# Pricing tile-size changes and holding small tiles in a build-time scheduler: a two-layer hybrid decoder on one Trainium2 core

## The chip, the cores and the metric

The kernel runs on one core of one Trainium2 chip. The metric is device time in microseconds, the median of three runs. TensorE (PE) multiplies, VectorE (DVE), ScalarE (ACT) and GpSimd (POOL) work elementwise, SyncE (SP) issues the DMAs. The kernel is one program with a queue of instructions for each engine. The order in each queue is fixed when the kernel is built, and semaphores make one engine wait for another.

## The reference

Two layers over a sequence of 512 tokens of width 1024, batch 1. Each layer is a mixer of three branches and a gated MLP with a short convolution, both between normalisations whose scales come from a condition `c` ("ada"):

```python
def token_mixer(h, ...):
    z = h @ w_in
    za, zb, zc, zg = split(z)
    y_a = nsa_attention(...)     # sparse: compressed, selected and window keys; 8 heads of 64
    y_b = mla_branch(...)        # low-rank q and kv, 8 heads of 96
    y_c = rwkv7_branch(...)      # recurrent state, 8 heads of 64, group norm
    g_a, g_b, g_c = split(sigmoid(zg))
    merged = g_a * (y_a @ w_a) + g_b * (y_b @ w_b) + g_c * (y_c @ w_c)
    return merged @ w_out

def conv_ffn(h, w_up, conv_w, conv_b, w_down):
    gate, val = split(causal_dwconv(h @ w_up, conv_w, conv_b))
    return (gelu(gate) * val) @ w_down

def reference(x, c, ...):
    for l in range(2):
        h = rms_norm(x, gain0) * (1 + sc1) + sh1
        x = x + gt1 * rms_norm(token_mixer(h, ...), gain1)
        h = rms_norm(x, gain2) * (1 + sc2) + sh2
        x = x + gt2 * rms_norm(conv_ffn(h, ...), gain3)
    return x
```

All arithmetic is float32.

## The kernel before, in words

**Two kinds of work.** The products with the weights (w_in, w_branch, w_out, ffn_up, ffn_down) form one long stream. A weight chunk is loaded by DMA (`rawt`), split by ACT (L507) and DVE (L476) into a high and a low half (`hlt`), and multiplied as three matmuls: high with high, high with low, low with high. These three are one stream operation; there are 2384 of them, and most of their matmuls have 512 columns. They run in one task, `master`, spawned under the name "gemm". Everything else is small: products of attention heads, of the RWKV pairs and of compression, most with 64 or 32 rows or columns, and the transposes (`tr`, L463, 128x128). Each stands in a task of its own: `mla_head` and `mla_pair`, `nsa_pair`, `rwkv_pair`, `pre` (normalise and transpose one of the four token tiles, 128 tokens each) and `post` (the residual step ahead of it).

**Tile sizes.** TensorE works in tiles of 128, 64 or 32 rows by 128, 64 or 32 columns, by the partitions of the stationary operand and by its width. The stream and the transposes use 128x128, the small products mostly 64x64, some 128x64, 64x128 and 32x32. In the profile the size stands behind the names (`64*64`).

**Who sets the order.** `Sched.run` simulates all engines while the program is built and picks one operation at a time. An operation's key begins with its earliest start (when its operands are ready by the planner's costs and its engine is free), then comes the task's priority (0 to 3 for small tasks, 9 for the stream: lower goes first), then its number. So a small product that the planner holds to be ready goes ahead of the stream, and the stream fills the rest. The costs (`pe`, L457, and `tr`) and the latencies between engines (`LAT`) are planned values; on the chip an engine waits when the planned order asks for something that is late.

**The places that matter here.** The stream is cut into units. Those of a branch ("BR") wait until all the branch's heads are done, by `yield ev("y", l, br)`; for MLA (branch 1) that is the end of the last `mla_pair`, and its first unit in layer 0 begins at stream operation 296 (B10 below), in layer 1 at 1504. `mla` spawns its heads two at a time, numbers 104 to 111 in layer 0; each takes four logits products, four row minima on DVE (`soft_head`, L1797), four exponentials on ACT, four normalisations on DVE (L485), transposes, and products with the values. In `rwkv_pair` the last pair ("rw3") ends with a chain of 128x512 elementwise steps on DVE (L476), then four transposes. `ada_block` makes the modulation vectors; three of its adds at a time run on POOL (L971). At the start of the MLP ("UP") and of layer 1, `post` and `pre` of the four token tiles feed the stream's first units (`first_units`: first the half with token tiles 0 and 1, then that with 2 and 3); the scaling by the norm is L1185, what leaves the transposes' PSUM bank is L1211 (ACT) and L1213 (DVE).

Of the kernel before, what the change touches and what calls it, by code (L numbers as in the profile page):

```python
# [58 lines left out]
class Ev:  # L59
    def __init__(self):  # L60
        self.deps = None


class Op:
    __slots__ = ("engs", "nbytes", "cols", "bank")

    def __init__(self, engs, nbytes=0, cols=0.0, bank=None):
        self.engs = engs
        self.bank = bank
        self.nbytes = nbytes  # L70
        self.cols = cols


class Cond:
    __slots__ = ("f",)
# [12 lines left out]
class Alloc:  # L88
    __slots__ = ("mem", "n", "cls", "job")
# [5 lines left out]
class Reserve:  # L95
    __slots__ = ("mem", "job")
# [111 lines left out]
}  # L208
FREE = 150.0


class Task:
    __slots__ = ("gen", "prio", "deps", "base", "req", "done", "name", "seq")
# [16 lines left out]
class Sched:  # L230


    def __init__(self):
        self.t = {e: 0.0 for e in ("PE", "ACT", "DVE", "POOL", "SP")}
        self.dma = 0.0
        self.tasks = []
        self.ticks = {}
        self.fill = None
        self.fill_t = 0.0
        self.cool = False  # L240
        self.past = []
        self.cur = None
        self.nseq = 0
        self.now = 0.0
        self.seen = {}
# [36 lines left out]
    def _step(self, k, val):  # L282
# [6 lines left out]
            k.req = None  # L289
        self.cur = prev  # L290

    TICK = 10240.0 / 3
    SHARE = 5000.0
    WARM = 3400.0
# [30 lines left out]
    def run(self):  # L325
        while self.tasks:
            best = None
            for k in self.tasks:
                r = k.req
                if type(r) is Op:  # L330
                    for e, c in r.engs:
                        st = max(k.at(e), self.t[e])
                        if r.bank in self.seen:

                            end, other = self.seen[r.bank]
                            if other != e:
                                st = max(st, end + LAT[other][e])
                        if k is self.fill and self.cool and (st > self.fill_t + self.SHARE or self.cooling(st)):
                            key = (st, -2, k.seq, 0.0)
                        elif len(r.engs) > 1:  # L340
                            key = (st, k.prio, k.seq, st + c)
                        else:
                            key = (st, k.prio, k.seq, 0.0)
                        if best is None or key < best[0]:
                            best = (key, k, e, c, st)
                    continue
                if type(r) is Ev:
                    if r.deps is None:
                        continue
                    st, e = max(k.ready(), max([t for t, g in r.deps])), None  # L350
                    key = (st, -1, k.seq, 0.0)
                elif type(r) is Cond:
                    if not r.f():
                        continue
                    st, e = max(k.ready(), self.now), None
                    key = (st, -1, k.seq, 0.0)
                elif type(r) is Reserve:
                    if not r.mem.reserve(r.job):
                        continue
                    st, e = max(k.ready(), self.now), None  # L360
                    key = (st, k.prio, k.seq, 0.0)
                else:
                    f = r.mem.find(r.n, r.cls, k.ready(), r.job)
                    if f is None:
                        continue
                    e, st = f
                    key = (st, k.prio - 0.5, k.seq, 0.0)
                if best is None or key < best[0]:
                    best = (key, k, e, 0.0, st)
# [6 lines left out]
            _, k, e, c, st = best  # L376
            self.now = max(self.now, st)
            r = k.req
            if type(r) is Op:
                end = self.pe_time(st, c, r.cols) if e == "PE" else st + c  # L380
                self.t[e] = end
                if r.bank is not None:
                    self.seen[r.bank] = (end, e)
# [23 lines left out]
def _fsz(ap):  # L407
    n = 1
    for s in ap.shape[1:]:
        n *= s  # L410
    return n
# [18 lines left out]
class Kern:  # L430
# [11 lines left out]
    def pe(self, mms, share=1.0):  # L442
        cost = cols = 0.0
        for out, lhsT, rhs, st, sp in mms:
            n, m = _fsz(rhs), _fsz(lhsT)
            if lhsT.dtype == FR:
                cost += max(n / 2.4, m / 1.2) + 3
                cols += n * lhsT.shape[0] * min(m, 128) / 16384
            else:
                c = max(n / 0.6, m / 0.684)  # L450
                if m <= 64:
                    c = (n / 0.6 + 47) / 2 if n > 16 else 53
                cost += c
                cols += 4 * n * lhsT.shape[0] * min(m, 128) / 16384
        yield Op([("PE", cost * share)], cols=cols)
        for out, lhsT, rhs, st, sp in mms:
            self.nc.tensor.matmul(out, lhsT, rhs, start=st, stop=sp)  # L457

    def tr(self, trs):
        cost = sum(0.85 * _fsz(ident) + 2 for _, _, ident in trs)  # L460
        yield Op([("PE", cost)], cols=sum(2 * _fsz(i) * i.shape[0] / 128 for _, _, i in trs))
        for out, in_, ident in trs:
            self.nc.tensor.transpose(out, in_, ident)  # L463

# [2308 lines left out]
```

## Time and profile before

| | |
|---|---|
| times of the runs | 2071.28, 2071.88, 2068.06 us, median 2071.28 |
| profiled execution | 2071.48 us, of which the span is 2069.4 us |
| mean granted TensorE clock | .994 |
| PE busy | 2019.6 us (98%) |
| DVE / ACT / POOL busy | 1340.3 / 998.2 / 292.2 us |
| PE's share of the chain that ended last | 88%, DVE 8% |
| largest group | L457 128x512 of `arenar,hlt`, 2880 matmuls, 711.7 us |

How to read it: the span is the time from the first instruction to the last; 2.1 us lie around it in this execution. A PE that is busy 98% is the bound, and what can be gained is what its queue loses: waits, changes of tile, and stretches at half clock (`PEclk` is the clock that was granted, 1.00 is full). Consecutive matmuls overlap, so the pace of a group is read from the starts of rows, not from the mean duration of one instruction.

### The profile page before, as it was taken

The numbers are of one execution on the slowest core, as the hardware profiler recorded it, in microseconds if no ns is written. First come the engines' busy times: TensorE is split into PE (matmuls) and PEld (weight loads), VectorE is DVE, ScalarE is ACT, GpSimd is POOL, SyncE is SP. The second block draws the span as 40 slices with busy tenths as digits, with TensorE's granted clock in tenths as the row PEclk, the third lists the DMA queues.
The fourth block names the chain that finished last, engine by engine and source line by source line (L and its number), as shares of the span: only waits on it lengthen the run. The fifth ranks groups of instructions, "written<-read, shape, count | busy, mean of one in ns | idle before, by whom it ended". The sixth has DMA issues, their size and how long they took to land.

```text
span 2069.4 us, 35607 instructions
## 1 busy us (share of the span) xinstructions
PE 2019.6 (98%) x14134; PEld 1638.0 (79%) x14134; DVE 1340.3 (65%) x2754; ACT 998.2 (48%) x1898; POOL 292.2 (14%) x268
## 2 busy tenths in 40 slices
PE   6999999999999999999999999999999999999998
PEld 4887777777788888888888777777777878888887
DVE  6687985677556766662467789765865676656423
ACT  4454652466445656541344456534754455444321
POOL 3001000340030234200010100004302211100000
PEclk9999999999999999999999999999999999999999
DMA  7532212441245355424422221224313544333342
GB/s 308 152 93 74 72 43 87 153 163 52 99 166 173 123 194 174 141 92 141 138 85 67 66 89 57 75 87 166 129 62 123 173 143 168 108 102 93 101 133 81
DMA packets 88423, 245.48 MB, mean 119 GB/s; under 512 B 24984, under 2 KB 26392, under 8 KB 87872
## 3 DMA queue, kind: packets, MB, share of 16 engines
q1 hardware_dynamic: 88256, 243.20, 35.3%
q8 instruction: 111, 1.82, 0.4%
q14 instruction: 56, 0.46, 0.1%
HBM read 233.19 MB, written 12.60 MB: 119 GB/s over the span
## 4 chain that ended last, share of the span: by engine, by line
PE 88%; DVE 8%; issue 1%; ACT 1%; DMA 1%; POOL 1%; DVEq 0%; POOLq 0%; SPq 0%; ACTq 0%
PE ps L457 83%; PE ps L463 4%; DVE xt L476 1%; DVE xt L485 1%; DVE arena L476 1%; DVE xt L1797 1%; DVE xt L480 1%; DVE hlt L476 1%; ACT xt L472 0%; POOL smallt L517 0%; DVE arena L480 0%; DVE arena L1213 0%; DMA arena<-rwd 0%; DVE xt L2561 0%; DMA rwd<-arena 0%
## 5 line engine op out<-in xcount | busy, mean ns | idle before, releaser
L457 PE MATMUL ps<-arenar,hlt 128*128 128x512 f32 (+1 forms) x2880 | 711.7, 396 | 1.6 <-DVE arenar L476 1.4
L457 PEld LDWEIGHTS ps<-arenar,hlt 128*128 128x128 f32 x2880 | 520.6, 190 | 109.1 <-issue 7.3
L476 DVE TENSOR_TENSOR hlt<-rawt,hlt 128x1024 fp32r<-128x1024 f32 (+2 forms) x260 | 312.6, 1202 | 371.1 <-ACT hlt L507 370.0
L457 PE MATMUL ps<-xt,hlt 128*128 128x512 f32 (+1 forms) x2208 | 477.5, 378 | 4.2 <-ACT arena L1211 4.2
L507 ACT CAST hlt<-rawt 128x1024 fp32r<-128x1024 f32 (+3 forms) x263 | 269.4, 1025 | 431.9 <-PE ps L457 323.0
L457 PEld LDWEIGHTS ps<-xt,hlt 128*128 128x128 f32 x2208 | 397.0, 190 | 81.0 <-ACT arena L1211 4.7
L457 PE MATMUL ps<-hlt,arenar 128*128 128x512 f32 (+3 forms) x1056 | 222.5, 365 | 0.0
L457 PEld LDWEIGHTS ps<-hlt,arenar 128*128 128x128 f32 x1056 | 185.4, 189 | 27.4 <-issue 1.0
L507 ACT COPY xt<-ps 128x512 f32<-128x512 f32 (+6 forms) x211 | 91.0, 476 | 91.6 <-PE ps L457 43.4
L480 DVE SCALAR_TENSOR_TENSOR yt<-ps,cpk,yt 128x511 f32<-128x511 f32 (+1 forms) x160 | 119.5, 747 | 3.3
L457 PE MATMUL ps<-xt 64*64 64x64 f32 (+11 forms) x1992 | 117.1, 258 | 4.3 <-ACT xt L472 2.4
L457 PEld LDWEIGHTS ps<-xt 64*64 64x64 f32 (+6 forms) x1992 | 84.2, 135 | 46.3 <-issue 31.4
L472 ACT ACTIVATE xt<-xt,smallt 128x512 f32<-128x512 f32 (+3 forms) x168 | 92.5, 552 | 55.8 <-DVE smallt L1797 55.7
L517 POOL TENSOR_TENSOR smallt<-smallt,mhalf 128x1 f32<-128x1 f32 (+2 forms) x56 | 58.5, 1049 | 276.3 <-DVE smallt L487 157.1
L457 PE MATMUL ps<-arenar 128*128 128x512 f32 x384 | 93.0, 390 | 0.0
L522 POOL TENSOR_SCALAR smallt<-smallt 128x1 f32<-128x1 f32 x20 | 5.1, 256 | 593.6 <-DVE smallt L487 582.6
L971 POOL TENSOR_TENSOR arena<-xt,arena 128x512 f32<-128x512 f32 x51 | 73.7, 1445 | 71.9 <-issue 36.7
L457 PEld LDWEIGHTS ps<-arenar 128*128 128x128 f32 x384 | 71.7, 188 | 14.7
L463 PE MATMUL ps<-kpack,xt 128*128 128x128 f32 x533 | 73.7, 275 | 6.2 <-DVE xt L476 4.5
L457 PE MATMUL ps<-hlt,xt 128*128 128x512 f32 x336 | 76.8, 389 | 0.0
L463 PEld LDWEIGHTS ps<-kpack,xt 128*128 128x128 f32 x533 | 61.1, 140 | 18.3 <-issue 3.7
L457 PEld LDWEIGHTS ps<-hlt,xt 128*128 128x128 f32 x336 | 63.1, 188 | 13.1
(264 smaller groups left out, 2490.4 us busy)
## 6 DMA issues: line engine op xcount, KB each, us to landing
rawt<-in_wch_dram SPq DMA_DIRECT2D x90, 512.0 KB, 3.5
rawt<-in_wup_dram SPq DMA_DIRECT2D x88, 512.0 KB, 3.5
rawt<-in_wdn_dram SPq DMA_DIRECT2D x44, 512.0 KB, 3.5
arena<-in_wada_dram SPq DMA_DIRECT2D x42, 512.0 KB, 5.2
xt<-in_wada_dram SPq DMA_DIRECT2D x33, 512.0 KB, 5.3
rawt<-in_wbr_dram SPq DMA_DIRECT2D x24, 512.0 KB, 3.5
yt<-in_wada_dram SPq DMA_DIRECT2D x21, 512.0 KB, 4.7
rawt<-in_wout_dram SPq DMA_DIRECT2D x16, 512.0 KB, 3.5
```

The lines of the kernel that those rows point to most:

```text
L457: self.nc.tensor.matmul(out, lhsT, rhs, start=st, stop=sp)
L463: self.nc.tensor.transpose(out, in_, ident)
L472: self.nc.scalar.activation(out, in_, func, bias=bias, scale=scale, **kw)
L476: self.nc.vector.tensor_tensor(out, a, b, op)
L480: self.nc.vector.scalar_tensor_tensor(out, a, s, b, op0, op1)
L485: self.nc.vector.tensor_scalar(out, a, s1, None, op0)
L507: self.nc.scalar.copy(out, in_)
L517: self.nc.gpsimd.tensor_tensor(out, in_, ex, OP.pow)
L522: self.nc.gpsimd.tensor_scalar(out, ss, a, b, OP.mult, OP.add)
L971: self.nc.gpsimd.tensor_tensor(a, w, a, OP.add)
L1797: nc.vector.tensor_tensor_reduce(dst, B3(o), B3(mask_ap(qt)), scale, 3.0e38, OP.add, OP.min, sm[:, qt:qt + 1])
```

## The change

The planner gets to know the tile size of each PE operation (`pe` works it out from the first product, `tr` is always 128x128) and keeps that of the last one in `self.tile`. Three things follow from it and one does not:

- An operation of another size than the last is charged 165 ns (CHANGE) in the planner's clock.
- While the last one was not full size, an operation of another size has 330 ns added to its key: small tiles of one size are held together. Where keys are equal, the one that needs no change goes first.
- A PE operation that is not of the stream counts as ready 150 ns later in its key (LATE). Its start in the planner's clock stays as it was.
- The planned cost of one stream matmul is n/2.4+13.4 ns instead of n/2.4+3, and its bound by weight loading is m/2.4 instead of m/1.2.

No instruction is added or taken away on PE: the program has 11225 matmuls and transposes in both. What changes is the order, and through it the buffers.

```diff
+FULL = (128, 128)
+CHANGE = 165.0
...
+    LATE = 150.0
...
+                        if e == "PE":
+
+                            new = r.tile != self.tile
+                            late = 2 * CHANGE if new and self.tile != FULL else 0.0
+                            if k is self.fill and self.cool and (st > self.fill_t + self.SHARE or self.cooling(st)):
+                                key = (st, -2, k.seq, 0.0)
+                            else:
+
+                                sure = st if k is self.fill else max(k.at(e) + self.LATE, self.t[e])
+                                key = (sure + late, k.prio, new, k.seq)
+                            if best is None or key < best[0]:
+                                best = (key, k, e, c, st)
+                            continue
+                        if len(r.engs) > 1:
...
-                end = self.pe_time(st, c, r.cols) if e == "PE" else st + c
+                if e == "PE":
+                    if r.tile != self.tile:
+                        st, self.tile = st + CHANGE, r.tile
+                    end = self.pe_time(st, c, r.cols)
+                else:
+                    end = st + c
...
-                cost += max(n / 2.4, m / 1.2) + 3
+                cost += max(n / 2.4, m / 2.4) + 13.4
...
+        size = lambda n: 128 if n > 64 else 64 if n > 32 else 32
+        tile = (size(mms[0][1].shape[0]), size(_fsz(mms[0][1])))
+        yield Op([("PE", cost * share)], cols=cols, tile=tile)
...
+        yield Op([("PE", cost)], cols=sum(2 * _fsz(i) * i.shape[0] / 128 for _, _, i in trs), tile=FULL)
```

In the whole PE order the tile size changes 401 times before and 373 times in the change. Three places show what moves. The line numbers are those of each kernel's own file (a matmul is L457 before and L481 in the change, a transpose L463 and L487); `ps_76` to `ps_83` are the eight PSUM banks, and x3 counts matmuls in a row.

First, PE in layer 0, the logits of the sparse branch against the compressed keys (64x31) and beside them stream operations (`arenar,hlt`). Before:

```order
L457 MATMUL ps_77<-arenar,hlt 128x512 x3
L457 MATMUL ps_78<-xt_104 32x32 x16
L457 MATMUL ps_79<-arena 64x31 x2
L457 MATMUL ps_79<-arena,xt_104 64x31 x2
L457 MATMUL ps_79<-arena 64x31 x4
L457 MATMUL ps_77<-arenar,hlt 128x512 x3
L457 MATMUL ps_79<-arena 64x31 x2
L457 MATMUL ps_79<-arena,xt_104 64x31 x2
L457 MATMUL ps_79<-arena 64x31 x4
```

The same kind of rows in the change, which stand later in the stream:

```order
L481 MATMUL ps_76<-arena,xt_104 64x31 x2
L481 MATMUL ps_76<-arena 64x31 x2
L481 MATMUL ps_78<-arenar,hlt 128x512 x3
L481 MATMUL ps_80<-arenar,hlt 128x512 x3
L481 MATMUL ps_79<-arena,xt_104 64x31 x2
L481 MATMUL ps_79<-arena 64x31 x2
```

The stream goes between the small products after a whole bank of them, two operations at a time, where before it went in after one.

Second, PE in layer 0 at the end of MLA. Before, its last products with the values (64x512 to 64x128) stand among stream operations, and 46 more stream operations lie between the last of them and B10:

```order
L457 MATMUL ps_78<-arena,xt_104 64x512 x2
L457 MATMUL ps_78<-arena,xt_104 64x384 x2
L457 MATMUL ps_78<-arena,xt_104 64x256 x2
L457 MATMUL ps_77<-arenar,hlt 128x512 x3
L457 MATMUL ps_76<-xt_104,arena 64x128 x2
L457 MATMUL ps_79<-xt_104,arena 64x128 x2
```

In the change; the first two rows are transposes of the last heads' softmax, the row with `ones` is a norm of rw3, and the last row is the first of B10:

```order
L487 MATMUL ps_83<-kpack,xt_104 128x128 x3
L487 MATMUL ps_79<-kpack,xt_104 128x128 x3
L481 MATMUL ps_76<-xt_104 64x512 x2
L481 MATMUL ps_76<-xt_104 64x384 x2
L481 MATMUL ps_78<-xt_104 64x512 x2
L481 MATMUL ps_79<-ones,arena 64x1 x8
L481 MATMUL ps_76<-xt_104 64x256 x2
L481 MATMUL ps_78<-xt_104 64x384 x2
L481 MATMUL ps_76<-xt_104 64x128 x2
L481 MATMUL ps_78<-xt_104 64x256 x2
L481 MATMUL ps_78<-xt_104 64x128 x2
L481 MATMUL ps_76<-arenar,hlt 128x512 x12
```

The second half of MLA (heads 108 to 111) has moved back by 56 stream operations on average, to the very end of its room; rw3 has moved forward by 22 on average and its last step from stream operation 313 to 296.

Third, PE at the start of the MLP in layer 0: transposes of token tiles (L463, L487) among the first UP units (128x256). Before:

```order
L457 MATMUL ps_76<-xt_5553,hlt 128x256 x24
L463 MATMUL ps_77<-kpack,arena 128x128 x2
L463 MATMUL ps_78<-kpack,arena 128x128 x2
L463 MATMUL ps_80<-kpack,arena 128x128 x2
L463 MATMUL ps_81<-kpack,arena 128x128 x2
L457 MATMUL ps_79<-xt_5553,hlt 128x256 x24
L457 MATMUL ps_77<-xt_5553,hlt 128x256 x9
L463 MATMUL ps_78<-kpack,arena 128x128 x2
```

In the change:

```order
L481 MATMUL ps_76<-xt_5554,hlt 128x256 x24
L487 MATMUL ps_77<-kpack,yt_5235 128x128 x2
L487 MATMUL ps_78<-kpack,yt_5235 128x128 x2
L487 MATMUL ps_79<-kpack,yt_5235 128x128 x2
L487 MATMUL ps_80<-kpack,yt_5235 128x128 x2
L481 MATMUL ps_81<-xt_5554,hlt 128x256 x3
L487 MATMUL ps_82<-kpack,yt_5235 128x128 x2
L487 MATMUL ps_83<-kpack,yt_5235 128x128 x2
L487 MATMUL ps_77<-kpack,yt_5235 128x128 x2
L481 MATMUL ps_81<-xt_5554,hlt 128x256 x3
L487 MATMUL ps_78<-kpack,yt_5235 128x128 x2
```

Of the four transposed tiles the third (t = 2) keeps its place behind 24 products; the fourth (t = 3) came after 33 more products and now comes after 3. It is the same in layer 1.

More of the change, by code (lines that the diff above doesn't have):

```diff
@@ L64, with __init__ @@
 class Op:
-    __slots__ = ("engs", "nbytes", "cols", "bank")
-    def __init__(self, engs, nbytes=0, cols=0.0, bank=None):
+    __slots__ = ("engs", "nbytes", "cols", "bank", "tile")
+    def __init__(self, engs, nbytes=0, cols=0.0, bank=None, tile=None):
         self.engs = engs
@@ L71, in __init__ @@
         self.cols = cols
+        self.tile = tile
 class Cond:
@@ L239, in __init__ @@
         self.fill_t = 0.0
+        self.tile = FULL
         self.cool = False
@@ L337, in run @@
                                 st = max(st, end + LAT[other][e])
-                        if k is self.fill and self.cool and (st > self.fill_t + self.SHARE or self.cooling(st)):
-                            key = (st, -2, k.seq, 0.0)
-                        elif len(r.engs) > 1:
+                        if e == "PE":
[10 more added lines that the diff above has]
+                        if len(r.engs) > 1:
                             key = (st, k.prio, k.seq, st + c)
@@ L454, in pe @@
                 cols += 4 * n * lhsT.shape[0] * min(m, 128) / 16384
-        yield Op([("PE", cost * share)], cols=cols)
+        size = lambda n: 128 if n > 64 else 64 if n > 32 else 32
+        tile = (size(mms[0][1].shape[0]), size(_fsz(mms[0][1])))
+        yield Op([("PE", cost * share)], cols=cols, tile=tile)
         for out, lhsT, rhs, st, sp in mms:
@@ L460, in tr @@
         cost = sum(0.85 * _fsz(ident) + 2 for _, _, ident in trs)
-        yield Op([("PE", cost)], cols=sum(2 * _fsz(i) * i.shape[0] / 128 for _, _, i in trs))
+        yield Op([("PE", cost)], cols=sum(2 * _fsz(i) * i.shape[0] / 128 for _, _, i in trs), tile=FULL)
         for out, in_, ident in trs:
```

## The prediction

> **What bounds the kernel now.** I read the page first, then PE's waits, then the chain and single stretches of the timeline.
>
> ```profile
> span 2069.4 us, 35607 instructions
> PE 2019.6 (98%) x14134; PEld 1638.0 (79%) x14134; DVE 1340.3 (65%) x2754; ACT 998.2 (48%) x1898; POOL 292.2 (14%) x268
> PE 88%; DVE 8%; issue 1%; ACT 1%; DMA 1%; POOL 1%; DVEq 0%; POOLq 0%; SPq 0%; ACTq 0%
> ```
>
> PE is the bound, and the change leaves its work as it is. It can win only where PE loses time: in tile changes, waits and half clock. The pace of the stream stands in the chain (start, us, count of matmuls):
>
> ```profile
> 554.48 114.49 PE ps L457 x506
> ```
>
> 114.49/506 = 0.226 us for each 128x512 matmul. What PE waited for in the whole span (total, times, longest):
>
> ```profile
> PE ps L463 <- DVE yt L1130: 10.7, 2, 7.8
> PE ps L463 <- DVE arena L1185: 6.9, 3, 2.6
> PE ps L463 <- DVE xt L476: 4.5, 4, 1.9
> PE ps L457 <- ACT arena L1211: 4.2, 2, 2.2
> ```
>
> The first row lies at the beginnings of the layers, rows two and four where the four token tiles enter the MLP and layer 1, row three at the ends of rw3. None of these lies in MLA: there the stream covers everything. So these waits are where a new order can take or give.
>
> **Tile changes.** The trace of before has excursions from the stream to 64x64 and back, a run inside 64x64, and one to transposes, which are full size:
>
> ```profile
> 182.49 0.33 PE L457 MATMUL ps<-arena 64*64 64x64 f32 x4
> 182.75 1.67 PE L457 MATMUL ps<-arenar,hlt 128*128 128x512 f32 x6
> 184.35 0.33 PE L457 MATMUL ps<-arena 64*64 64x64 f32 x4
> ...
> 210.91 1.63 PE L457 MATMUL ps<-arenar,hlt 128*128 128x512 f32 x6
> 212.37 0.60 PE L463 MATMUL ps<-kpack,arena 128*128 128x128 f32 x4
> 212.73 2.32 PE L457 MATMUL ps<-arenar,hlt 128*128 128x512 f32 x9
> ...
> 273.15 0.33 PE L457 MATMUL ps<-xt 64*64 64x64 f32 x4
> ...
> 274.44 0.33 PE L457 MATMUL ps<-xt,arena 64*64 64x64 f32 x4
> ```
>
> From 182.49 to 184.35 lie 1.86 us, six stream matmuls take 1.36, so four small records with both changes take 0.50. Inside a run the same four take 0.117 (273.15 to 274.44, twelve rows, eleven steps). A round trip costs 0.38, one change 0.19. The transposes show that the size counts: 210.91 to 212.73 is 1.82, less 1.36 is 0.46 for four, 0.115 each, with nothing left for a change. The order has 401 changes before and 373 after. 28 x 0.19 = **−5.2**. I keep −4 for the end of the range, since 18 of the 28 are changes between small sizes, which no row above prices.
>
> The Trainium skill ("TensorEngine Tiling (Array Packing)", Key Properties) says that a change of tiling mode drains TensorE. The 0.38 agrees; by this rule every change costs about the same, and the sum by it is the one above.
>
> **rw3's end, both layers.** In layer 0 and in layer 1 PE stands before rw3's transposes:
>
> ```profile
> 391.51 2.30 PE L457 MATMUL ps<-arenar,hlt 128*128 128x512 f32 x9
> 395.76 0.63 PE L463 MATMUL ps<-kpack,xt 128*128 128x128 f32 x4 [1.95 <-DVE xt L476]
> ...
> 1418.43 0.66 PE L463 MATMUL ps<-kpack,xt 128*128 128x128 f32 x4 [1.94 <-DVE xt L476]
> ```
>
> Why DVE is late there shows in layer 1, in POOL's and DVE's rows side by side:
>
> ```profile
> 1410.10 4.67 POOL L971 TENSOR_TENSOR arena<-xt,arena 128x512 f32<-128x512 f32 x3
> 1410.16 1.77 DVE L476 TENSOR_TENSOR xt<-xt,smallt 128x512 f32<-128x512 f32 x1 [1.54 <-POOL smallt L517]
> 1411.96 3.35 DVE L476 TENSOR_TENSOR xt<-xt 128x512 f32<-128x512 f32 x2
> 1415.95 0.69 DVE L476 TENSOR_TENSOR xt<-xt 128x512 f32<-128x512 f32 x1
> ```
>
> Three 128x512 steps took 5.1 us while POOL added, one took 0.69 afterwards. The first wait is followed by half clock (us, then PE, PEld, DVE, ACT, POOL, PEclk, DMA share, GB/s):
>
> ```profile
> 386.00:393.00 7.00, 7.00 (x37) 5.93 (x36) 6.93 (x7) 3.00 (x5) 4.63 (x4) 1.00 0.23 75
> 396.00:403.00 7.00, 7.00 (x34) 5.55 (x33) 0.32 (x2) 0.74 (x1) 0.00 (x0) 0.53 0.79 299
> ```
>
> 7 x (1.00 − 0.53) = 3.3 us lost. In the change rw3 ends 17 stream operations earlier in layer 0 and 47 earlier in layer 1, there ahead of POOL's adds. Layer 0: −1.95 − 3.3 = **−5.25**. Layer 1: −1.95, less 0.5 for what a shorter wait may leave, **−1.45**.
>
> **MLA's end in layer 0.** B10 waits for all heads, and its place in the stream hasn't moved (378 us in the trace of before), but the 46 stream operations (46 x 3 x 0.226 = 31 us) that stood between MLA's end and B10 are gone. Heads 108 to 111 now run straight into it, and nothing stands behind them on PE until B10. So their softmax on DVE has to keep up. PE's side, from the first logits to head 110's transposes: the logits by these rows,
>
> ```profile
> 227.48 5.85 PE L457 MATMUL ps<-yt 96*128 96x384 f32 x20
> 232.97 1.05 PE L457 MATMUL ps<-arenar,hlt 128*128 128x512 f32 x3
> ```
>
> 5.49 us for 20 records, 0.27 each, 32 records for four heads 8.8; 27 stream matmuls 6.1; 21 transposes 2.4; one rw3 product 0.8. Together 18.1. DVE's side, up to head 110's normalisation:
>
> ```profile
> L476 DVE TENSOR_TENSOR hlt<-rawt,hlt 128x1024 fp32r<-128x1024 f32 (+2 forms) x260 | 312.6, 1202 | 371.1 <-ACT hlt L507 370.0
> L485 DVE TENSOR_SCALAR xt<-xt,smallt 128x128 f32<-128x128 f32 (+3 forms) x168 | 63.1, 423 | 0.5
> L1797 DVE CUSTOM_DVE_ANT_0 xt<-ps,arena 128x512 f32<-128x512 f32 (+1 forms) x104 | 45.5, 484 | 27.1 <-PE ps L457 27.0
> ```
>
> 16 minima x 0.484 = 7.7; 12 normalisations x 0.423 = 5.1; eight 128x512 steps of rw3 x 0.69 = 5.5; two low halves x 1.2 = 2.4; small ones about 2. Together 22.7. That is 4.6 behind PE, and 2.4 if a tenth of DVE's durations overlaps. Head 111 comes again behind that with 0.6 to 2, and B10's first bank is free only after MLA's last copy, about 1 more. So 2 to 8, and I take **+5**, above the middle of PE's two sides since rw3's chain has waits of its own that I count at nothing. If PE stands for 5 us, half clock may follow: one of the two 1.95 waits above had it, so half of 3.3, **+1.65**. Nothing below zero is possible here: before there was no wait. The stream operations that stood there move ahead and cover other small work, so they lose nothing. In layer 1 MLA still ends 26 stream operations (18 us) ahead of its unit, and I count nothing.
>
> What speaks against this place is the pair of rows above on rw3: three of its steps beside one set of POOL's adds took 5.1 us instead of 3 x 0.69 = 2.1. If one set falls on the steps that now run beside MLA's softmax, DVE is 3 us later still.
>
> The Trainium skill ("SBUF — State Buffer", SBUF: two separate sides) has a rule for this: DVE operations with two operands in SBUF and GpSimd's share a port pair as an exclusive lock, and the loser stands still for the whole instruction. The 5.1 us agree. By the rule no order of these instructions on DVE's queue alone would help, and only rw3's distance in time from POOL's adds counts; the sum by it is the same plus those 3 us.
>
> **The MLP's start, both layers.** Before, on PE and on DVE:
>
> ```profile
> 677.46 3.13 PE L457 MATMUL ps<-xt,hlt 128*128 128x256 f32 x24 [1.96 <-ACT arena L1211]
> 682.73 1.56 PE L463 MATMUL ps<-kpack,arena 128*128 128x128 f32 x8 [2.14 <-DVE arena L1185]
> 683.95 5.37 PE L457 MATMUL ps<-xt,hlt 128*128 128x256 f32 x33
> ...
> 684.82 1.41 DVE L480 SCALAR_TENSOR_TENSOR arena<-arena,smallt 128x512 f32<-128x512 f32 x2
> 688.43 0.48 DVE L1185 TENSOR_SCALAR arena<-arena,smallt 128x512 f32<-128x512 f32 x1
> ```
>
> PE reaches tile 2's transposes early and waits 2.14, then 33 products cover tile 3, whose scaled rows are ready at 688.9. In the change tile 3's transposes come after 3 products (0.4 us), at about 684.3. If DVE stayed, PE would wait 4.6. It doesn't quite: tile 3's scaling now stands ahead of tile 2's copies on DVE, so it can be ready by about 684.82 + 1.41 + 2 x 0.48 = 687.2, a wait near 3; and the 30 products put back cover tile 2's and 3's copies later, some 1 us. **+2** each, 0 to 4, so **+4**.
>
> **Small things.** At the change of layers twelve products instead of six cover the last token tile, and its transposes come two operations earlier: −0.5 (−1.5 to +0.5). A wait of 150 ns in the key shifts other small products behind the stream and shortens the many waits under 1 us: −1 (−2 to 0). The cost constant for stream matmuls (n/2.4+13.4 at 512 columns is .227, the row above .226) makes the planner's clock truer; its effect is in the positions already counted. DVE, ACT and the DMA queue get the same instructions in another order.
>
> **Sum.** −5.2 − 5.25 − 1.45 + 5 + 1.65 + 4 − 0.5 − 1 = −2.75. The profiled execution took 2071.48 (span 2069.4 and 2.1 around it), 0.2 over the median 2071.28; 2071.48 − 2.75 = 2068.7, and I name that.
>
> **Rivals.** About 0.2% or 4.1 us is what a measurement of this kernel can tell from no change.
>
> *The new waits are covered* (faster). DVE runs ahead of PE at MLA's end because head by head the softmax starts with the first logits, and UP's wait only moves from tile 2 to tile 3. Then +5, +1.65 and +4 fall away: 2071.5 − 13.4 = 2058, or 2062 with half of the UP waits. For it: DVE is busy 65% and none of PE's waits above lies in MLA. Against: that was with the stream between.
>
> *MLA's end is a real hole* (slower). The place is PE before B10 in layer 0. If one set of POOL's adds lies beside rw3's steps, the 5 become 8, or 11 from the upper end of 8; I take 9, the half clock of 3.3 behind it, and UP at +3 each: −5.2 − 6.7 − 1.5 + 9 + 3.3 + 6 = +4.9, 2076; with a dearer UP (+4 each) and tile changes at −4 it is 2080. It decides from a hole of 11.5 us on, half clock included (4.1 + 13.4 of gains, less 6 for UP): below that the gains hold it within 0.2%.
>
> *Merging saves nothing* (the change doesn't do what it says). If small-to-small changes are free, 28 changes fewer are five round trips fewer (185 to 180), 5 x 0.38 = 1.9 instead of 5.2: 2072.
>
> **Chances.** Forecast as summed, 2064 to 2073: .45, of which .13 below 2067.2 and .32 within 0.2%. Covered waits .26, all faster. The hole .21, of which .19 beyond 2075.4. No saving .08, of which .06 within. Faster .39, same .40, slower .21. The range takes the unknown ends: low −5.2 − 5.25 − 1.95 − 1.5 − 1 = −14.9 with nothing new, 2057; high as in the hole with dear UP, 2080.
>
> **What would show it.** Tile changes: round trips at the same .38, fewer of them, PE busy about 3 to 5 us less. rw3: the two waits on DVE L476 gone, and PEclk 1.00 around 396 us. MLA: a wait of 2 to 8 us near 375 us ahead of `arenar,hlt`, on DVE's normalisation or ACT's copy. UP: a wait of about 3 us at tile 3's transposes near 684 and 1700, on DVE L1185's successor. I am wrong if PE has no wait before B10 (then faster), or if one over 9 us stands there (then slower), or if rw3's end is late again for another reason.

## The result and the profile after

The changed kernel takes 2093.69 us (2092.94 to 2094.91, four runs), the kernel before 2071.58 (both the median of all four runs; later sets have four or more). The ratio is 1.0112, interval 1.0100 to 1.0124: 22 us slower. The forecast was 2068.7, with 2057 to 2080 as its range. The profiled execution took 2094.17 us, and its span is 23.0 us longer than before.

The page of the changed kernel, the lines that answer to those of before:

```profile
span 2092.4 us, 35619 instructions
PE 2027.3 (97%) x14134; PEld 1642.6 (79%) x14134; DVE 1337.7 (64%) x2755; ACT 997.6 (48%) x1897; POOL 290.0 (14%) x268
```

The work of every engine is the same within 8 us. PE's waits (total, times, longest), the larger rows of the list:

```profile
PE ps L487 <- DVE yt L1154: 10.8, 2, 7.9
PE ps L481 <- DVE arena L500: 5.8, 3, 2.2
PE ps L481 <- DVE xt L504: 3.9, 4, 1.7
PE ps L487 <- DVE xt L535: 3.5, 3, 3.0
PE ps L487 <- DVE yt L1209: 3.0, 3, 1.4
...
PE ps L487 <- DVE arena L535: 2.0, 1, 2.0
PE ps L487 <- DVE yt L1237: 2.0, 1, 2.0
PE ps L481 <- DVE xt L2600: 1.8, 2, 1.4
PE ps L487 <- DVE arena L500: 1.7, 1, 1.7
```

The whole list, which leaves out waits under 0.15 us, adds up to 58.1 us in 49 waits, before to 42.9 in 30. The first row, the start of the program, is as before; the row for rw3's end (`xt` L476 before, 4.5 us) is down to 0.4 us further down the list; the others are new places or tile rows of the MLP's start.

To split the 23 us I set every step from one PE record to the next against the median that the trace of before has for that shape behind the same predecessor. An excess over 0.14 us counts as a wait, and smaller ones inside windows at half clock count as half clock. Waits 41.9 before, 61.1 after: **+19.2**. Half clock 8.0 and 14.8: **+6.8**. All else 2004.9 and 2001.8: **−3.1**. Together +22.9.

These parts are rough. h1 below is the same program as e1 and comes out 1.1 us higher in waits and 2.7 higher in half clock. Two figures of the profile itself agree in direction: the listed waits grow by 15.2 us, and the mean granted clock falls from .994 to .991, which is 6.4 us of full speed (0.006 x 2069.4 = 12.4, 0.009 x 2092.4 = 18.8).

Where it arose shows when the start of the same stream operation is set side by side in the two traces. At operation 449, in the mixer of layer 0, the change is 14.3 us behind; the MLP of layer 0 brings it to 18.1, the mixer of layer 1 to 21.6, the last MLP to 23.0.

### The profile page after: what moved, and what is told of

Same layout as the page of the kernel before. It is cut to its first block, busy times and chain, and to the rows that moved or that the text cites. A ratio compares the mean times of both kernels' runs of the same rounds, so it can differ in the third digit from the quotient of the medians.

```text
span 2092.4 us, 35619 instructions
## 1 busy us (share of the span) xinstructions
PE 2027.3 (97%) x14134; PEld 1642.6 (79%) x14134; DVE 1337.7 (64%) x2755; ACT 997.6 (48%) x1897; POOL 290.0 (14%) x268
## 5 line engine op out<-in xcount | busy, mean ns | idle before, releaser
L481 PE MATMUL ps<-arenar,hlt 128*128 128x512 f32 (+1 forms) x2880 | 713.1, 397 | 3.3 <-DVE arenar L500 2.3
L481 PEld LDWEIGHTS ps<-arenar,hlt 128*128 128x128 f32 x2880 | 522.4, 191 | 121.8 <-issue 15.9
L481 PE MATMUL ps<-xt,hlt 128*128 128x512 f32 (+1 forms) x2208 | 479.3, 378 | 3.4 <-ACT xt L531 1.5
L481 PEld LDWEIGHTS ps<-xt,hlt 128*128 128x128 f32 x2208 | 397.8, 190 | 80.9 <-issue 1.9
L481 PE MATMUL ps<-hlt,arenar 128*128 128x512 f32 (+3 forms) x1056 | 222.1, 364 | 0.0
L481 PEld LDWEIGHTS ps<-hlt,arenar 128*128 128x128 f32 x1056 | 184.3, 189 | 27.6 <-issue 1.2
L531 ACT COPY xt<-ps 128x512 f32<-128x512 f32 (+5 forms) x207 | 86.4, 465 | 123.8 <-PE ps L487 67.8
L496 ACT ACTIVATE xt<-xt,smallt 128x512 f32<-128x512 f32 x192 | 105.8, 552 | 77.2 <-DVE smallt L1821 74.8
L995 POOL TENSOR_TENSOR arena<-arena 128x512 f32<-128x512 f32 x42 | 62.2, 1480 | 353.1 <-ACT arena L496 334.9
L481 PE MATMUL ps<-xt 64*64 64x64 f32 (+8 forms) x1868 | 106.5, 265 | 3.2 <-DVE xt L2600 1.4
L481 PEld LDWEIGHTS ps<-xt 64*64 64x64 f32 (+3 forms) x1868 | 73.3, 134 | 37.1 <-issue 26.6
L481 PE MATMUL ps<-arenar 128*128 128x512 f32 x384 | 93.3, 390 | 0.0
L487 PE MATMUL ps<-kpack,xt 128*128 128x128 f32 x591 | 82.6, 282 | 7.5 <-DVE xt L535 3.5
L487 PEld LDWEIGHTS ps<-kpack,xt 128*128 128x128 f32 x591 | 69.2, 144 | 19.4 <-DVE xt L535 4.8
L481 PEld LDWEIGHTS ps<-arenar 128*128 128x128 f32 x384 | 71.8, 188 | 14.8
L1821 DVE CUSTOM_DVE_ANT_0 xt<-ps,arena 128x512 f32<-128x512 f32 (+3 forms) x144 | 64.6, 483 | 24.1 <-PE ps L481 24.0
L481 PE MATMUL ps<-hlt,xt 128*128 128x512 f32 x336 | 76.8, 389 | 0.0
```

The lines of the kernel that those rows point to most:

```text
L496: self.nc.scalar.activation(out, in_, func, bias=bias, scale=scale, **kw)
L531: self.nc.scalar.copy(out, in_)
L995: self.nc.gpsimd.tensor_tensor(a, w, a, OP.add)
L1821: nc.vector.tensor_tensor_reduce(dst, B3(o), B3(mask_ap(qt)), scale, 3.0e38, OP.add, OP.min, sm[:, qt:qt + 1])
```

## Experiments

The medians of before in the sets of e1 to h2 lay between 2069.65 and 2070.87 us, and each ratio is to before in the same set. "Waits" and "half clock" are those of the split above, of the profiled execution of each kernel; "changes" counts tile changes in the order. The execution of p1 that was profiled was its longest (2075.91).

| run | us | ratio, interval | changes | waits | half clock |
|---|---|---|---|---|---|
| before | 2071.58 | 1 | 401 | 41.9 | 8.0 |
| the change | 2093.69 | 1.0112, 1.0100–1.0124 | 373 | 61.1 | 14.8 |
| e1 hold only | 2061.24 | .9955, .9941–.9968 | 365 | 37.6 | 9.1 |
| e2 price only | 2085.74 | 1.0078, 1.0057–1.0099 | 370 | 61.1 | 11.3 |
| e3 LATE only | 2102.56 | 1.0157, 1.0138–1.0177 | 606 | 44.0 | 5.4 |
| e4 cost only | 2074.79 | 1.0022, 1.0011–1.0033 | 390 | 47.5 | 11.0 |
| f1 change, PE x 0.93 | 2069.50 | 1.0000, .9989–1.0010 | 381 | 46.4 | 8.6 |
| f2 change, DVE, ACT x 1.1 | 2082.96 | 1.0068, 1.0052–1.0084 | 383 | 55.2 | 9.8 |
| f3 before, PE x 1.07 | 2078.66 | 1.0047, 1.0029–1.0066 | 389 | 50.9 | 6.5 |
| f4 change, no price | 2079.68 | 1.0049, 1.0032–1.0066 | 367 | 55.5 | 11.2 |
| n1 change, LATE 140 | 2077.59 | 1.0036, 1.0022–1.0050 | 376 | 49.6 | 11.1 |
| n2 change, CHANGE 150 | 2068.75 | .9992, .9983–1.0001 | 365 | 47.1 | 8.7 |
| m1 before, PE x 0.93 | 2071.42 | 1.0005, .9996–1.0014 | 376 | 48.1 | 7.9 |
| g1 hold, PE x 0.95 | 2076.21 | 1.0025, 1.0015–1.0035 | 362 | 52.4 | 10.3 |
| p1 change, DVE lightened | 2071.82 | 1.0006, .9996–1.0015 | 373 | 49.1 | 7.3 |
| p2 before, DVE lightened | 2060.51 | .9949, .9935–.9964 | 401 | 34.0 | 6.8 |
| p3 change, POOL's adds small | 2078.95 | 1.0042, 1.0027–1.0057 | 373 | 52.1 | 10.1 |
| p4 before, POOL's adds small | 2055.51 | .9925, .9911–.9940 | 401 | 31.2 | 6.8 |
| h1 hold 300 ns | 2061.32 | .9950, .9934–.9967 | 365 | 38.7 | 11.8 |
| h2 hold, adds on DVE | 2052.24 | .9911, .9896–.9925 | 391 | 33.6 | 5.4 |

**The parts alone (e1 to e4).** First theory: the old plan's PE ran faster than the chip's, which left cover that nobody counted, and the change took it away ("lost cover"). Rival: any other order of this plan waits more or less, whatever the rule ("chance"). Each part was put into the kernel before by itself (only the lines that matter are shown, here and below):

```diff
 e1, against the kernel before
+    late = 2 * CHANGE if new and self.tile != FULL else 0.0
 e2
+    if r.tile != self.tile:
+        st, self.tile = st + CHANGE, r.tile
 e3
+    sure = st if k is self.fill else max(k.at(e) + 150.0, self.t[e])
 e4
-    cost += max(n / 2.4, m / 1.2) + 3
+    cost += max(n / 2.4, m / 2.4) + 13.4
```

> The kernel before with the hold alone (330 ns in the key of an operation of another size, and fewer changes at equal keys); no LATE, no change priced in the planner's clock, the old cost of stream matmuls. The order has 365 tile changes against 401, so 36 x 0.19 = 6.8 us less on PE. Lost-cover theory (the change took away slack that the old plan had without counting it, and the chip turned it into waits): the hold lets small products go ahead of the stream up to 330 ns before their operands are there, so PE waits 3 to 8 us more, time 2067 to 2073. Chance theory (any other order of this plan waits more than the one of before, whatever the rule): waits rise by 8 to 20 us, time 2073 to 2085.

> The kernel before with 165 ns charged to the planner's PE clock at each tile change, and fewer changes at equal keys; no hold, no LATE, the old cost of stream matmuls. 370 tile changes against 401: -5.9 us. Lost-cover theory: the clock becomes truer, about 0.33 us of uncounted cover per excursion goes, PE's waits rise by 5 to 12 us, time 2071 to 2078. Chance theory: waits rise by 8 to 20 us as in the other runs, time 2074 to 2086.

> The kernel before with LATE = 150 ns alone, and fewer changes at equal keys. The order has 606 tile changes against 401: 205 x 0.19 = +39 us on PE. Lost-cover theory: the cover grows, so PE's waits fall by 3 to 6 us from those of before; time 2104 to 2109. Chance theory: waits rise by 8 to 20 us here too, time 2118 to 2130.

> The kernel before with the new planned cost of stream matmuls alone (n/2.4+13.4 instead of n/2.4+3, which is 227 instead of 216 ns at 512 columns). 390 tile changes against 401: -2.1 us. Lost-cover theory: 5% of every cover goes, 0.03 us for each stream operation between, so PE's waits rise by 2 to 6 us, time 2071 to 2076. Chance theory: waits rise by 8 to 20 us, time 2077 to 2089.

The hold alone comes out below both ranges, faster than both kernels, with waits 4.3 below those of before. The price alone has the waits of the whole change, more than lost cover allowed. LATE alone comes out below both ranges too. It has no fewer waits (44.0), so 150 ns more in the key buy no cover in this order; what it costs is 205 more tile changes, and all but waits and half clock is 32.6 us over before, 0.16 each. Only e4 is where lost cover put it. The rival in its first form, waits 8 to 20 us higher whatever the rule, holds for e2 alone. By these four the price looks like the cause.

**The pace of the plan (f1 to f4).** If lost cover is the cause, the plan's pace should steer the waits, with the tile price and without. I added a third reading, that the price groups small work ("bunching").

```diff
 f1, against the change; f3, against the kernel before, with 1.07
     def pe_time(self, st, c, cols):
+        c = 0.93 * c
 f2
-                    end = st + c
+                    end = st + (1.1 * c if e in ("DVE", "ACT") else c)
 f4
-                        st, self.tile = st + CHANGE, r.tile
+                        self.tile = r.tile
```

> The changed kernel with every planned PE duration multiplied by 0.93 (the charge of 165 ns for a tile change stays as it is). Lost-cover theory, now in proportion to time: the old plan's PE ran about 7% faster than the chip's (10 ns on each of 7408 stream matmuls, and 401 tile changes of 0.19 us uncounted: 74 + 76 = 150 of 2069 us), so DVE and ACT had 7% more time than planned for all they do in a busy stretch; the priced plan took that away. Giving it back brings PE's waits down by 12 to 19 us: 2072 to 2082. Bunching theory (the price at a change groups small work, and the groups arrive where nothing covers them, whatever the pace): waits stay, 2090 to 2098. Chance theory: anything between 2070 and 2100.

> The changed kernel with every planned DVE and ACT duration multiplied by 1.1. Lost-cover theory: the plan leaves DVE and ACT a tenth more time, so PE's waits fall by 6 to 15 us: 2078 to 2088. Bunching theory: waits stay, 2090 to 2098. Chance theory: anything between 2070 and 2100.

> The kernel before, which knows no tile sizes, with every planned PE duration multiplied by 1.07: the pace of the plan becomes the chip's, with no price on a tile change, no hold and no LATE. 389 tile changes against 401: -2.3 us. Lost-cover theory: PE's waits rise by 10 to 20 us: 2078 to 2090. Bunching theory: waits stay, 2066 to 2072. Chance theory: anything between 2065 and 2090.

> The changed kernel without the 165 ns charged to the planner's clock; hold, LATE and the new cost of stream matmuls stay. 367 tile changes against 401: -6.5 us. Lost-cover theory: half of the 7% is left (the 76 us of tile changes), so waits are those of the run with the new cost alone, 5 to 9 us over before: 2067 to 2075. Bunching theory: the waits of the hold alone, 2059 to 2066. Chance theory: anything between 2058 and 2085.

f2 and f3 fall into the ranges of lost cover, f1 2.5 us below its range and f4 4.7 above. Bunching holds none of the four. But chance in its wider form allows f2, f3 and f4 and misses f1 by 0.5 us, and with the price gone f4 still has 55.5 us of waits.

**Neutral changes (n1, n2) and more cover (m1, g1).** These ask how much the time moves when nothing of substance changes.

```diff
 n1, against the change
-    LATE = 150.0
+    LATE = 140.0
 n2, against the change
-CHANGE = 165.0
+CHANGE = 150.0
 m1, against the kernel before; g1, against e1, with 0.95
     def pe_time(self, st, c, cols):
+        c = 0.93 * c
```

> The changed kernel with LATE = 140 instead of 150 ns, a change that means nothing. 376 tile changes (373). If the waits are a property of the rules (lost-cover theory), the time stays within 6 us of the change: 2088 to 2100. If they are an accident of one order (chance theory), this run or the next lies more than 8 us from 2093.7, anywhere from 2070 to 2105.

> The changed kernel with CHANGE = 150 instead of 165 ns (and so the hold at 300): nearly neutral, a tenth of the price is gone. 365 tile changes (373): -1.5 us. Lost-cover theory: 2085 to 2097. Chance theory: this run or the one before lies more than 8 us from 2093.7, anywhere from 2070 to 2105.

> The kernel before with every planned PE duration multiplied by 0.93: no tile sizes, and the plan's PE now runs about 14% faster than the chip's instead of 7%. 376 tile changes against 401: -4.8 us. Lost-cover theory: more cover, waits fall by 0 to 6 us: 2060 to 2067. Chance theory: 2062 to 2085, waits can rise as well.

> The hold alone (no price, no LATE, old cost of stream matmuls) with every planned PE duration multiplied by 0.95: hold and more cover together. 362 tile changes against 365 with the hold alone. Lost-cover theory: waits as with the hold alone or 0 to 5 us less: 2055 to 2062. Chance theory: 2056 to 2080.

Chance wins in all four, though n2 lies a little over 1 us below the range that was given. Ten nanoseconds of LATE take 16 us off the change, 15 ns of CHANGE take 25 us off, and n2 has all of the change's rules and the time of the kernel before. More cover did not help before (waits 48.1 instead of 41.9) and cost the hold 15 us. The orders are far apart for it: PE's order has some 2500 rows in n2 and in the change, the two part at the 130th row, and most rows behind it differ. These four lie some 0, 15, 16 and 25 us from the kernel that each of them varies. By that estimate, single-part runs of this planner can't be read as causes below about 20 us: e2's 16 us may be the price, and may be its order.

**The same order with one resource relieved (p1 to p4).** What can be read is a kernel whose order stays exactly as it is while one engine's instructions get shorter; the planned costs are left alone.

```diff
 p1, p2 (m is 8 after the first use of a slot)
-                yield from self.tt(ch["lo"], ch["rawap"], ch["hi"], OP.subtract)
+                yield Op([("DVE", 1.045 * n + 66)])
+                self.nc.vector.tensor_tensor(ch["lo"][:, 0:m], ch["rawap"][:, 0:m], ch["hi"][:, 0:m], OP.subtract)
 p3, p4
-                    self.nc.gpsimd.tensor_tensor(a, w, a, OP.add)
+                    self.nc.gpsimd.tensor_tensor(a[:, 0:8], w[:, 0:8], a[:, 0:8], OP.add)
```

> The changed kernel, every engine's order exactly as it is, but DVE's low halves of the weight chunks (hlt, 128x1024, 1.2 us each, 260 of them, 312 of DVE's 1340 us) are cut to 8 columns after the first use of each slot: it leaves out most of the low-half split, so the products use stale low halves. Late-DVE theory (the extra waits of the change are DVE behind its plan in busy stretches): most of the 19 us of extra waits goes, 2072 to 2080, and the difference to the kernel before in the same state shrinks to 12 us or less. Chain theory (products stand behind each other with nothing between, so PE sees the latency of a chain whatever DVE's load): 2085 to 2092, and the difference stays at 18 to 24.

> The kernel before with the same cut of the low halves to 8 columns, order unchanged. Late-DVE theory: 2061 to 2067 (of its 14 us of waits inside the layers and at the units' starts, some 5 to 9 go). Chain theory: 2066 to 2070.

> The changed kernel, order unchanged, but POOL's adds for the modulation (L995, 128x512, 1.48 us, 42 of them) work on 8 columns: it leaves out most of these sums. It takes away POOL's hold on DVE and nothing else. Late-DVE theory with POOL as the main cause: the wait at MLA's end (normalisations 3.02 us instead of 1.33 beside POOL) and those at 399 us go, with half clock behind them: 2080 to 2088. If POOL is a small part: 2088 to 2093.

> The kernel before, order unchanged, with POOL's adds on 8 columns. Both waits at rw3's end (1.95 us each) and the half clock behind the first (3.3 us) should go, by the reading in the prediction: 2063 to 2066. If rw3's end is late for another reason: 2069 to 2071.

All four come out below every range that was given, by 0.2, 0.5, 1.1 and 7.5 us.

DVE's load: lightened by 253 us (1337.7 to 1084.5 busy), the change gains 21.9 us and the kernel before 11.1 (with 254 us less). The difference between the two shrinks from 22.1 to 11.3. So half of the 22 us hangs on DVE's load, that is, on DVE running late in the new order; the other half stays even with DVE half idle (52% busy). What goes lies in the mixer of layer 0: at its end p1 is some 6.5 us behind p2, where the change was 14.3 behind the kernel before. The places can be followed. Rows with a wait in the change, then the same rows in p1:

```profile
150.79 3.66 PE L481 MATMUL ps<-arena,xt 64*64 64x64 f32 x64 [2.20 <-DVE arena L500]
265.83 0.66 PE L487 MATMUL ps<-kpack,arena 128*128 128x128 f32 x4 [2.05 <-DVE arena L535]
343.58 0.33 PE L481 MATMUL ps<-xt,arena 64*64 64x64 f32 x4 [1.33 <-DVE xt L504]
401.69 0.30 PE L481 MATMUL ps<-arena 64*64 64x31 f32 x4 [1.42 <-DVE arena L500]
```

```profile
148.85 2.13 PE L481 MATMUL ps<-arena,xt 64*64 64x64 f32 x64 [0.60 <-DVE arena L500]
259.31 0.65 PE L487 MATMUL ps<-kpack,arena 128*128 128x128 f32 x4 [0.96 <-DVE arena L535]
334.31 0.33 PE L481 MATMUL ps<-xt,arena 64*64 64x64 f32 x4 [0.38 <-DVE xt L504]
389.22 0.30 PE L481 MATMUL ps<-arena 64*64 64x31 f32 x4 [0.96 <-DVE arena L500]
```

All four shrink and none goes, which looks like a late DVE on top of a chain with too little between. They don't have one cause, though. In p3 the first three stay (2.36, 2.03 and 1.32 us), and the fourth is gone, so that one is POOL's:

```profile
393.89 0.30 PE L481 MATMUL ps<-arena 64*64 64x31 f32 x4
```

For the first one DVE's own row in the change names what held it, a round trip through DRAM that stands in its queue ahead of the step PE needs:

```profile
148.65 0.69 DVE L500 TENSOR_TENSOR xt<-xt,kpack 128x512 f32<-128x512 f32 x1 [4.66 <-DMA xt<-rwd]
```

In p1 DVE still waits 4.35 us for that trip, but its step comes 1.9 us earlier, while PE's stretch ahead of the wait ends only 0.3 earlier.

POOL's adds: they cost 14.7 us in the change and 14.5 to 16.1 before (2055.51 against 2069.98 in its own set, or against 2071.58). So POOL isn't the difference (without the adds the kernels lie 23.4 us apart), though its adds fall on other places in each. It is dear in both, twice the 7.2 us that the prediction read off the two waits at rw3's end and the half clock. The expectations named one group of 42 adds; L995 (L971 before) has 141 adds in all, p3 and p4 cut all of them, and POOL's busy time falls from 290.0 to 132.0 in p3. Their results come earlier too, but that can't be much of the gain: in the trace of before the one wait of another engine that an add ends is 0.4 us long. PE's rows at rw3's end in p4, both layers:

```profile
390.26 2.30 PE L457 MATMUL ps<-arenar,hlt 128*128 128x512 f32 x9
392.40 0.60 PE L463 MATMUL ps<-kpack,xt 128*128 128x128 f32 x4
...
1406.79 0.60 PE L463 MATMUL ps<-kpack,xt 128*128 128x128 f32 x4
```

The two waits of 1.95 are gone, and the stretch behind the first runs at full clock (20 us, columns as in the prediction):

```profile
386.00:406.00 20.00, 20.00 (x108) 16.65 (x108) 7.15 (x10) 8.31 (x12) 1.55 (x7) 1.00 0.55 192
```

That confirms the reading of these rows in the prediction.

**The last two (h1, h2).** Is the hold's gain its own, and can POOL's 14 us be had in a kernel that computes everything?

```diff
 h1, against e1
-    late = 2 * CHANGE if new and self.tile != FULL else 0.0
+    late = 300.0 if new and self.tile != FULL else 0.0
 h2, against e1
-    ADA_ENG = ("DDDDDDPP", "PPDGDDGD", "DDDDDDDD", "DDDDDDDD", "GGGGGGGG")
+    ADA_ENG = ("DDDDDDPP", "PPDGDDGD", "DDDDDDDD", "DDDDDDDD", "DDDDDDDD")
```

> The hold alone with 300 instead of 330 ns, a nearly neutral change of the run with the hold alone (2061); 365 tile changes as there. If the hold itself is worth what that run showed (6.8 us of tile changes and waits no worse than before): 2058 to 2066. If 2061 was a lucky order: 2067 to 2082, as in the run of the hold with a plan 5% faster (2076).

> The hold alone, and the modulation sums that ACT and POOL made together (42 adds of 1.48 us on POOL) made by DVE alone, 0.69 us each, in a new order; everything is computed. POOL's hold on DVE cost 14 to 15 us in both kernels with the order unchanged. If it goes and DVE's 33 us more are hidden: 2046 to 2056. If DVE's load gives half of it back: 2056 to 2064. The scatter between orders, 8 us either way, lies over both.

h1 tells less than planned: with 300 ns the planner makes exactly the order of e1, so 2061.32 is a repeat of 2061.24 and no second draw. Whether the hold's 8 to 9 us are its own stays open; of them, 6.4 are neither waits nor half clock (7.9 in h1), where 36 changes fewer at e3's 0.16 would be 5.8. h2 takes 2052.24, .9911 of before, inside its range: the fastest of all that compute everything, and faster than both kernels. It moved 140 of POOL's instructions, not 42. DVE works 64 us more than before, POOL 202 less, and ACT 100 less:

```profile
PE 2011.0 (98%) x14134; PEld 1635.9 (80%) x14134; DVE 1404.2 (68%) x2910; ACT 898.1 (44%) x1742; POOL 90.0 (4%) x128
```

It has a new order too, so its 9 us against e1 carry the scatter of orders; that its gain has the sign of p4's 14.5, with the order fixed, makes POOL's adds the likely cause, not a shown one. ACT's lighter load is a rival that no run separates.

## Why the prediction was wrong

**Tile changes (−5.2).** Right in direction; the size isn't shown. All but waits and half clock (span less the two) is 3.1 us less, for 28 changes fewer. That remainder moves for other reasons too: against before it is 5.3 less in e4 with 11 changes fewer, and 9.0 less in f1 with 20 fewer. Only e3 is large enough to price a change. Of its 205 more, 194 go to or from full size, and 32.6 us are 0.16 for each change, or 0.34 for a round trip where the prediction read 0.38; at 0.16 the 28 are worth 4.5 us. The rival that merging saves nothing among small sizes is not settled. In e1 26 of the 36 changes fewer touch full size, which is 4.9 us by the rival and 6.8 by the prediction; 6.4 was measured, and 7.9 in h1, the same program. PE's busy time, which was to fall by 3 to 5 us, rose by 7.7; matmuls at half clock count longer in it (x20 below takes 4.53 us at half clock, 2.98 in p3 at full clock), so it doesn't settle the point either.

**rw3's end (−5.25 and −1.45).** Right. Both waits are gone, what is left before its transposes is small, and the clock behind them is full (1.00 from 429 to 440 us):

```profile
429.74 0.63 PE L487 MATMUL ps<-kpack,xt 128*128 128x128 f32 x4 [0.42 <-DVE xt L500]
...
1514.69 2.15 PE L487 MATMUL ps<-kpack,xt 128*128 128x128 f32 x16 [0.23 <-DVE xt L535]
```

**MLA's end in layer 0 (+5 and +1.65).** Right in place; that the size nearly agrees is luck. PE's rows in the change, DVE's normalisations at the same time, and the clock:

```profile
371.22 0.55 PE L487 MATMUL ps<-kpack,xt 128*128 128x128 f32 x3 [0.75 <-DVE smallt L1821]
374.76 4.53 PE L487 MATMUL ps<-kpack,xt 128*128 128x128 f32 x20 [2.99 <-DVE xt L535]
...
385.11 3.70 PE L481 MATMUL ps<-arenar,hlt 128*128 128x512 f32 x15 [0.76 <-DVE arenar L500]
```

```profile
371.08 3.02 DVE L509 TENSOR_SCALAR xt<-xt,smallt 128x128 f32<-128x128 f32 x4
```

```profile
370.00:380.00 10.00, 6.26 (x31) 5.11 (x32) 9.21 (x21) 7.27 (x21) 5.90 (x4) 0.66 0.18 52
```

Waits of 4.5 us, and 10 x (1 − 0.66) = 3.4 us of half clock: 7.9 where 6.65 stood. But POOL's adds ran beside the last normalisations. The forecast counted no adds here; its rival of a real hole put one set of them beside rw3's steps. In p3, in the same place of the same order, the four steps take 1.26 us, two waits are left of three, and the clock is full:

```profile
368.17 1.26 DVE L509 TENSOR_SCALAR xt<-xt,smallt 128x128 f32<-128x128 f32 x4
```

```profile
370.09 2.98 PE L487 MATMUL ps<-kpack,xt 128*128 128x128 f32 x20 [1.24 <-DVE xt L535]
...
378.75 3.74 PE L481 MATMUL ps<-arenar,hlt 128*128 128x512 f32 x15 [0.76 <-DVE arenar L500]
```

```profile
365.00:385.00 20.00, 17.94 (x166) 13.67 (x166) 11.41 (x33) 13.60 (x33) 2.72 (x8) 1.00 0.49 187
```

So without the adds, softmax that falls behind on DVE, the mechanism of the forecast, leaves 2.0 us and no half clock. That is the lower end of its 2 to 8; the other 5.9 us hang on POOL's adds.

**The MLP's start (+4).** Near in size (3.7 and 1.4, together 5.1), but not by the rows that the prediction named, so luck has a part in it. By the starts of stream operations layer 0 loses the 3.7 and layer 1 the 1.4. In layer 0 the largest piece is a wait of 1.99 before it begins, in the units of w_out, where a token tile's transposes now stand earlier than their bank is free:

```profile
684.00 0.44 PE L487 MATMUL ps<-kpack,arena 128*128 128x128 f32 x2 [1.99 <-DVE yt L1237]
...
692.31 1.27 PE L487 MATMUL ps<-kpack,yt 128*128 128x128 f32 x8 [1.02 <-ACT yt L1207]
695.13 4.66 PE L481 MATMUL ps<-xt,hlt 128*128 128x256 f32 x24 [1.55 <-ACT xt L531]
700.50 1.09 PE L487 MATMUL ps<-kpack,yt 128*128 128x128 f32 x8 [0.71 <-DVE yt L1209]
...
703.34 1.14 PE L487 MATMUL ps<-kpack,yt 128*128 128x128 f32 x6 [1.39 <-DVE yt L1209]
```

Tile 3's transposes wait 1.39, not 3, and tile 2's 0.71 instead of 2.14.

**The change of layers (−0.5).** Right: −0.5 by the stream's starts.

**Small things (−1).** This is the step that failed. The terms above, as measured, make about −3.1 − 6.5 + 7.9 + 5.1 − 0.5 = +2.9. The other 20 us are new waits and the half clock behind them inside the two mixers, at places that the prediction did not look at: the four rows shown with p1, and in layer 1, among others,

```profile
1187.09 0.34 PE L481 MATMUL ps<-arena,xt 64*64 64x64 f32 x4 [2.13 <-DVE arena L500]
...
1308.07 1.32 PE L487 MATMUL ps<-kpack,xt 128*128 128x128 f32 x8 [1.74 <-DVE arena L500]
...
1505.05 0.44 PE L481 MATMUL ps<-yt,arenar 128*128 128x128 f32 x2 [1.36 <-DVE smallt L1821]
```

With DVE lightened (p1) the first and the last of these stay, at 2.44 and 1.36 us, and the second falls to 0.68.

The prediction worked out the places where the order had visibly moved and put the rest, where most rows had moved too, at −1 with bounds of −2 and 0. The only reason given was what 150 ns more in the key should do, and in e3 it didn't do it (44.0 us of waits, 41.9 before). Nothing bounded the rest from above. n1, n2 and g1 show what bound was needed: orders made by nearly the same rules lie 15 to 25 us apart. n2, with the same four rules, takes 2068.75, within 0.1 us of the forecast, which is luck: it is another order. So the loss belongs to this order and not to the rules as such, and a forecast for this order was possible only by following each product in it. The rival for "slower" named one place (MLA's end), and that place gave a third of the loss.

**Slips in the working.** 28 x 0.19 is 5.3, not 5.2, and DVE's 22.7 less a tenth is 2.3 behind PE, not 2.4. The first row of PE's waits lies at the start of the program alone, not at the beginnings of both layers. None of these changes the forecast by more than 0.1 us.

**What stays open.** Why half of the 22 us remains with DVE lightened. Chains with too little between are what the rows in p1 look like, but no run put stream operations back between them with all else kept. Nor is it shown that the price, the hold or LATE shifts the mean over many orders, apart from LATE's tile changes in e3.

## What to carry to other kernels

Where a planner writes the order, a change of its rules draws a new order, and one time is one draw: run two or three variants that mean nothing (here 140 for 150) before a rule is praised or blamed, and give a forecast at least that spread. To find what an order loses, keep it and shorten one resource's instructions with the planned costs untouched: four such runs told here where the time goes, which twelve runs with new orders could not. Nor was a truer clock of the planner a better plan by itself (e4 2074.79, f3 2078.66), though both lie within the scatter; what no plan here modelled (POOL's hold on DVE) fell where nothing covered it.

## What was unexpected of the hardware

POOL's modulation adds cost 14.5 us of the kernel before with the order unchanged, though the prediction had found only two waits behind them. DVE's 128x512 steps in that group took 845 ns on the mean before and 684 in p4:

```profile
L476 DVE TENSOR_TENSOR xt<-xt 128x512 f32<-128x512 f32 x19 | 16.1, 845 | 0.2
```

```profile
L476 DVE TENSOR_TENSOR xt<-xt 128x512 f32<-128x512 f32 x19 | 13.0, 684 | 0.2
```

Short DVE steps are held too. Beside two adds a 128x62 step with one tensor operand and one with two took 1.29 and 1.33 us, where the same kinds had taken 0.19 and 0.22 just before. Each ends within 0.1 us of the add beside it:

```profile
397.49 0.19 DVE L511 TENSOR_SCALAR arena<-arena 128x62 f32<-128x62 f32 x1
397.71 0.22 DVE L500 TENSOR_TENSOR arena<-arena 128x62 f32<-128x62 f32 x1
398.46 1.75 POOL L995 TENSOR_TENSOR arena<-arena 128x512 f32<-128x512 f32 x1 [5.93 <-ACT arena L496]
...
398.98 1.29 DVE L511 TENSOR_SCALAR arena<-arena 128x62 f32<-128x62 f32 x1
400.29 1.26 POOL L995 TENSOR_TENSOR arena<-xt,arena 128x512 f32<-128x512 f32 x1
400.31 1.33 DVE L500 TENSOR_TENSOR arena<-arena 128x62 f32<-128x62 f32 x1
```

In p3, with the adds cut and the order the same, these two steps take 0.20 and 0.22 us:

```profile
392.67 0.20 DVE L511 TENSOR_SCALAR arena<-arena 128x62 f32<-128x62 f32 x1
392.90 0.22 DVE L500 TENSOR_TENSOR arena<-arena 128x62 f32<-128x62 f32 x1
```

The port rule of the Trainium skill ("SBUF — State Buffer", SBUF: two separate sides) names DVE operations with two operands in SBUF, and those in a two-port mode, which it says `tensor_scalar` can enter. The trace agrees for the step with two operands (1.33 us instead of 0.22), and the `tensor_scalar` with one tensor operand stood as long. Whether that one runs in such a mode no run here shows.
